# Small loads moved from POOL's queue to ACT's and SP's, and 26 shared slots where there were 24

## The chip, the cores and the metric

The kernel runs on one core of a Trainium2 chip. The metric is the device time of one execution in microseconds (us), the median of several runs. The core has five engines with instruction streams of their own: TensorE (PE; its weight loads are shown as PEld), VectorE (DVE), ScalarE (ACT), GpSimd (POOL) and SyncE (SP). Each stream runs in order. A load from memory is issued by an instruction of one of these streams and carried out by 16 DMA engines that all of them share; the issuing engine goes on meanwhile. In the profile, SPq or ACTq is the issuing side of an engine.

## What is computed

Two layers of a decoder on 256 tokens of 1024 features, in float32. Each layer is a mixer of three attention branches (A, B, C), gated and summed, an output projection and a layer norm, and then a mixture of 32 experts of which each token uses two, with a second layer norm:

```python
for l in range(DEPTH):
    mix = token_mixer(x, w_in[l], q_norm_g[l], w_uq[l], kv_norm_g[l], w_ukv[l], w_gate[l],
                      b_gate[l], w_a[l], w_b[l], w_c[l], w_o[l], cos_m, sin_m, cos_p, sin_p)
    x = layer_norm(alpha * x + mix, ln1_g[l], ln1_b[l])
    ffn = hier_moe(x, w_group[l], b_group[l], w_sub[l], b_sub[l], w1[l], w3[l], w2[l])
    x = layer_norm(alpha * x + ffn, ln2_g[l], ln2_b[l])
# token_mixer: merged = g0 * (o_a @ w_a) + g1 * (o_b @ w_b) + g2 * (o_c @ w_c); return merged @ w_o
# hier_moe: for e in range(32): y += combine[:, e] * ((silu(t @ w1[e]) * (t @ w3[e])) @ w2[e])
```

The expert weights are 3 MB each, 96 MB a layer, and all of them are read.

## The kernel before

**Slots.** Most of the on-chip memory is a pool of NSLOT = 24 slots (line 48) of 8 KiB on each of 128 partitions, which the stream of weights shares with the large temporaries of the mixer (class Slots, from line 116). One slot holds 1 MB, a whole weight tile of an expert.

**The weights' stream.** Ring (from line 166) has all weights in the order of their use. A first, dry pass over the program notes how many slots the temporaries hold after each change and where each weight is last used. In the real pass `pump` issues the next weight (L195, or L193 where a tile is gathered from four experts) as soon as `fits` finds that until the weight's last use no more than NSLOT slots would be held. All of them are issued from SP. The program's order is the order in which the Python code is written out: a load stands on SP's stream at the place at which `pump` issued it, and waits there for whoever used its slot last.

**The stages.** `setup` (line 294) issues nine loads from SP: the first part of the constants, the first half of x, the first weight, the second half of x, three more weights, the rest of the constants, and the masks (L326). Then it calls `load_small(0, ...)`, and then has ACT load a function table (L1356, `self.table`). The mixer's first actions follow: transposes of x (L519), their split into a high and a low part (L278 on ACT, L279 on DVE), the split of the first weights by the same two lines, and the first products (L283 to L285).

**Experts.** `moe` goes through the 32 experts in eight steps of four (e = 0, 4, ... 28). A step multiplies gathered rows by w1 and w3 (L1691), then by w2 (L1771), and gathers the rows of the next step (L1650). After each kind of product its weights' slots are given back, and `pump` issues more weights there. In layer 0 the end of step e = 8 calls `load_small(1, ...)` for the next layer; the router's weights go to a slot taken for them (tile wr). At e = 16, `overflow` (L1860) holds three loads of SP in a branch that is taken only when an expert has more than 32 tokens; the branch isn't taken here. Also at e = 16 of layer 0, `small_T` and `small_rows` use what load_small(1) has brought. At the end of e = 20, `load_gains` fetches the gain and the bias of the second norm into a slot of their own (tile gb, L449).

**Small loads.** load_small (from line 398) clears a tile of vectors (L402, on POOL) and issues eleven loads: seven of vectors into it (L403 to L410), the router's weights w_group and w_sub behind other data of a slot or into a slot of their own (L413, L414; rows of 16 and 128 bytes), and two biases (L416, L417). L1326 issues two loads of 4 KB (tile gpk) some way ahead of the experts. All of these, and load_gains, issue from POOL.

Of the kernel before, what the change touches and what calls it, by code (L numbers as in the profile page):

```python
# [44 lines left out]
# Columns of the output projection, and of the last experts' second product: the last ones are few, as a norm waits for them.  # L45
WO = [(0, 512), (512, 256), (768, 256)]

NSLOT = 24
T1 = 5

# Splits of weights run so many pieces ahead of their products.
# [4 lines left out]
# The steps of the last layer's end.  # L56
# [5 lines left out]
# The piece by which a queue of attention steps is to be through, and the tensor work left for what lies between two steps.  # L62
# [53 lines left out]
class Slots:  # L116
    """8 KiB slots that the weight stream and the large temporaries share."""
# [23 lines left out]
    def part(self, name, n):  # L141
        """One of n parts of a slot."""
        for p in self.shared[n]:
            if p["free"]:
                return Part(self, n, p, p["free"].pop())
        p = {"tile": self.alloc([P, n, 2048 // n], F32, name), "free": set(range(1, n))}
        self.shared[n].append(p)
        return Part(self, n, p, 0)
# [17 lines left out]
class Ring:  # L166
    """Weights in the order of their use, each loaded as soon as a slot can be spared until then.

    `plan` is what a dry pass over the program has found: the slots that its temporaries hold after
    each change, and the change at which each weight tile is released."""  # L170
# [43 lines left out]
class Dry:  # L214
    """Stands for every object of the language in the dry pass."""
# [13 lines left out]
class Trunk:  # L229
# [27 lines left out]
    def tap(self, name, ap):  # L257
        if name in self.dbg:
            self.nc.gpsimd.dma_start(self.dbg[name], ap)
# [5 lines left out]
    def evac(self, out, in_, n):  # L265
        """PSUM to SBUF on the engine of the two that has less to do."""
# [7 lines left out]
    def split(self, hi, lo, src, n):  # L274
        """src = hi + lo exactly, each of 12 significant bits."""
# [11 lines left out]
    def warm(self, n, src):  # L287
        """Products that nobody reads: the tensor engine's clock falls to half when it has little to do."""
# [109 lines left out]
    def load_small(self, l, home, o):  # L398
        """The layer's vectors, off the weights' queue; the router's weights behind the first o floats of a slot."""
        nc, a = self.nc, self.a  # L400
        v = self.v = self.t([P, P], F32, "vec", 1)
        nc.gpsimd.memset(v, 0.0)  # L402
        nc.gpsimd.dma_start(v[0:2], a["q_norm_g"][l].rearrange("(k p) -> k p", p=P))  # L403
        nc.gpsimd.dma_start(v[2:3], a["kv_norm_g"][l:l + 1])
        nc.gpsimd.dma_start(v[3:27], a["b_gate"][l].rearrange("(k p) -> k p", p=P))
        nc.gpsimd.dma_start(v[27:35], a["ln1_g"][l].rearrange("(k p) -> k p", p=P))
        nc.gpsimd.dma_start(v[35:43], a["ln1_b"][l].rearrange("(k p) -> k p", p=P))
        m = max(l - 1, 0)
        nc.gpsimd.dma_start(v[43:51], a["ln2_g"][m].rearrange("(k p) -> k p", p=P))
        nc.gpsimd.dma_start(v[51:59], a["ln2_b"][m].rearrange("(k p) -> k p", p=P))  # L410
        self.wgs = home
        self.wgb = home[:, o:o + KD * 72].rearrange("p (k f) -> p k f", k=KD)
        nc.gpsimd.dma_start(self.wgb[:, :, 36:40], a["w_group"][l].rearrange("(k p) f -> p k f", p=P))  # L413
        nc.gpsimd.dma_start(self.wgb[:, :, 40:72], a["w_sub"][l].rearrange("(k p) f -> p k f", p=P))  # L414
        self.br = self.t([1, 36], F32, "br", 1)
        nc.gpsimd.dma_start(self.br[:, 0:4], a["b_group"][l:l + 1])  # L416
        nc.gpsimd.dma_start(self.br[:, 4:36], a["b_sub"][l:l + 1])  # L417

    def small_T(self):
        """The vectors with their features on partitions; the router's weights with the gain of its input taken in."""  # L420
# [14 lines left out]
    def small_rows(self):  # L435
        """Sums over the features: what a token's mean and the input's bias add to its logits."""
# [9 lines left out]
    def load_gains(self, l, which, rows=P):  # L446
        gb = self.slots.alloc([P, 2, D], F32, "gb")
        for j, n in enumerate(("g", "b")):
            self.nc.gpsimd.dma_start(gb[:rows, j], self.a[f"ln{which}_{n}"][l:l + 1].broadcast_to([rows, D]))  # L449
        return gb  # L450

    def spread_gains(self, gb):
        """The first partition's rows to all."""
# [8 lines left out]
    def step(self, f, need=None, cost=0.45, key=None, after=()):  # L462
        """An attention step: what it needs marked, its tensor time, and steps that must lie some tensor time back."""
# [18 lines left out]
    def run_fg(self, budget):  # L482
        """Attention steps worth so much tensor time, the most urgent first."""
# [7 lines left out]
    def run_fg_until(self, mark):  # L491
        """Everything of a branch that is left, other branches' steps where it would wait."""
# [6 lines left out]
    def rate(self, i):  # L499
        """Tensor time of attention steps that a piece must be joined by for all to be done when due."""  # L500
# [29 lines left out]
    def pieces(self, l):  # L530
        """The mixer's dense products in order: each is (key of its weights, last use, prepare, product)."""
# [67 lines left out]
        def gates(br, q):  # L599
            """Two 128-column tiles of a branch's gate."""  # L600
# [26 lines left out]
        def outp(br, w, kt, i, need):  # L627
            """A branch's output columns, gated and summed: 256 or 512 columns at a time."""
# [108 lines left out]
    def rope(self, v, t, nh, half, c, s):  # L737
        """Rotates the leading dims of [128, heads, dims] in place."""
# [13 lines left out]
    # -- branch A --  # L752
# [73 lines left out]
    # -- attention units: (block 0, four heads) or (block 1, two heads), 512 scores a row --  # L826
# [1123 lines left out]
```

## Time and profile before

| | before |
|---|---|
| median of 3 runs | 1023.01 us (1022.1 to 1024.78) |
| span of the profiled execution | 1022.9 us |
| TensorE busy | 955.5 us, 93% |
| DVE, ACT, POOL busy | 473.9, 416.6, 161.7 us |
| loaded from memory | 282.44 MB, 277 GB/s over the span |

The profile is of one execution. Its page gives the busy time of each engine, the span cut into 40 slices with a digit for the busy share of each (9 is 90% or more), and the chain of work that ended last, followed back from the end. Other views of the same trace list instructions in order of time with the idle time ahead of them and what ended it, sum up waits, or cut the trace into stretches. Times in the trace are counted from the start of the span. The mixer of layer 0 runs to about 290 us, its experts to about 500; layer 1 takes the same steps from there.

### The profile page before, as it was taken

Reading aid. Unit: us, or ns where it says so; the run is one execution under the profiler, and the core shown is the slowest. Engines: PE = TensorE matmul, PEld = TensorE weight load, DVE = VectorE, ACT = ScalarE, POOL = GpSimd, SP = SyncE. Lnnn points to the kernel's source line nnn. Section 1 sums busy time; section 2 is a strip of 40 time slices with the busy share of each in tenths; the row PEclk is TensorE's granted clock in tenths of the full one; section 3 lists DMA queues with packets and bytes.
Section 4 is the critical chain, followed back from the end, with each engine's and each line's share of the span. In section 5 each row is a group of like instructions: output and inputs, shape, how many; then the busy total and the mean of one; then the engine's idle time right before and its main releaser. Section 6 shows DMA issues by size and latency. Waiting matters only on the chain.

```text
span 1022.9 us, 18674 instructions
## 1 busy us (share of the span) xinstructions
PE 955.5 (93%) x7584; PEld 770.8 (75%) x7591; DVE 473.9 (46%) x968; ACT 416.6 (41%) x911; POOL 161.7 (16%) x274
## 2 busy tenths in 40 slices
PE   8999999999999997879879999999999999977794
PEld 7888899899986774556469888998999867654462
DVE  5747776845642110111398586676455420101014
ACT  5545646644442221112345646665354422211131
POOL 4531210021100110000156071000311000000001
PEclk9999999999999998889989999999999999989898
DMA  9933261696969999999992134426968799999993
GB/s 330 328 103 124 79 210 42 220 340 216 365 241 380 417 400 419 418 417 375 376 340 68 64 124 128 162 90 224 330 232 321 288 379 420 419 419 417 419 370 121
DMA packets 100170, 284.76 MB, mean 278 GB/s; under 512 B 6324, under 2 KB 53808, under 8 KB 78576
## 3 DMA queue, kind: packets, MB, share of 16 engines
q1 hardware_dynamic: 99088, 283.12, 73.7%
q8 instruction: 62, 1.02, 0.4%
q0 software_dynamic: 992, 0.39, 0.2%
q14 instruction: 28, 0.23, 0.1%
HBM read 282.44 MB, written 1.05 MB: 277 GB/s over the span
## 4 chain that ended last, share of the span: by engine, by line
PE 68%; DMA 17%; issue 7%; POOL 3%; DVE 3%; SPq 1%; ACT 1%; POOLq 0%; DVEq 0%; ACTq 0%
DMA w<-in_w_dram 15%; PE bank L283 12%; PE bank L284 12%; PE bank L285 12%; PE bank L1650 7%; PE bank L1691 7%; PE bank L837 3%; PE bank L1771 3%; DMA w<-in_w_in_dram 2%; PE bank L891 2%; PE bank L878 2%; PE bank L1757 1%; PE bank L840 1%; PE bank L1459 1%; DVE xTl L279 1%
## 5 line engine op out<-in xcount | busy, mean ns | idle before, releaser
L279 DVE TENSOR_TENSOR ws<-w,ws 128x1024 fp32r<-128x1024 f32 (+2 forms) x154 | 184.7, 1208 | 133.1 <-ACT ws L278 124.2
L278 ACT ACTIVATE ws<-w 128x1024 fp32r<-128x1024 f32 (+2 forms) x158 | 159.0, 1023 | 35.5 <-PE bank L285 15.9
L1691 PE MATMUL bank<-w,xg 128*32 128x256 f32 x2048 | 139.6, 413 | 33.9 <-DMA w<-in_w_dram 24.4
L1691 PEld LDWEIGHTS bank<-w,xg 128*32 128x32 f32 x2048 | 70.2, 118 | 105.1 <-DMA w<-in_w_dram 30.5
L1650 PEld LDWEIGHTS bank<-xg,x 128*128 128x128 f32 x512 | 124.2, 334 | 3.0 <-issue 2.5
L1650 PE MATMUL bank<-xg,x 128*128 128x128 f32 x512 | 125.7, 399 | 0.0
L283 PE MATMUL bank<-ws,xTh 128*128 128x408 f32 (+3 forms) x320 | 116.6, 364 | 1.2 <-ACT xTh L278 1.2
L1654 ACT ACTIVATE xg<-bank,gpk 128x128 f32<-128x128 f32 x128 | 51.7, 454 | 159.3 <-PE bank L1650 159.3
L283 PE MATMUL bank<-xTh,ws 128*128 128x256 f32 x384 | 111.2, 290 | 0.0
L285 PE MATMUL bank<-ws,xTl 128*128 128x408 f32 (+3 forms) x320 | 110.6, 346 | 0.6 <-DVE xTl L279 0.6
L284 PE MATMUL bank<-ws,xTh 128*128 128x408 f32 (+3 forms) x320 | 110.3, 345 | 0.0
L284 PE MATMUL bank<-xTl,ws 128*128 128x256 f32 x384 | 108.6, 283 | 0.0
L285 PE MATMUL bank<-xTh,ws 128*128 128x256 f32 x384 | 108.5, 283 | 0.0
L1721 DVE SCALAR_TENSOR_TENSOR t<-t,cw,bank 128x256 f32<-128x256 f32 x16 | 10.8, 677 | 157.2 <-PE bank L1691 157.2
L283 PEld LDWEIGHTS bank<-xTh,ws 128*128 128x128 f32 x384 | 73.5, 191 | 1.8 <-issue 1.0
L284 PEld LDWEIGHTS bank<-xTl,ws 128*128 128x128 f32 x384 | 73.6, 192 | 0.2
L285 PEld LDWEIGHTS bank<-xTh,ws 128*128 128x128 f32 x384 | 73.5, 191 | 0.0
L283 PEld LDWEIGHTS bank<-ws,xTh 128*128 128x128 f32 x320 | 61.4, 192 | 8.1 <-ACT xTh L278 1.8
L853 ACT ACTIVATE p<-bank,nb 128x128 f32<-128x128 f32 (+1 forms) x92 | 37.3, 420 | 69.9 <-DVE nb L845 65.1
L285 PEld LDWEIGHTS bank<-ws,xTl 128*128 128x128 f32 x320 | 61.0, 191 | 5.9 <-DVE xTl L279 1.6
L284 PEld LDWEIGHTS bank<-ws,xTh 128*128 128x128 f32 x320 | 61.3, 192 | 3.4 <-DVE ws L279 0.3
L1771 PE MATMUL bank<-w,t 128*32 128x512 f32 (+1 forms) x544 | 59.1, 571 | 1.0 <-DVE t L272 1.0
(361 smaller groups left out, 1530.2 us busy)
## 6 DMA issues: line engine op xcount, KB each, us to landing
w<-in_w_dram SPq DMA_DIRECT2D x168, 1024.0 KB, 15.7
w<-in_w_gate_dram SPq DMA_DIRECT2D x24, 1024.0 KB, 5.3
w<-in_w_dram SPq DMA_DIRECT2D x80, 256.0 KB, 7.2
w<-in_w_in_dram SPq DMA_DIRECT2D x18, 1024.0 KB, 7.7
w<-in_w_in_dram SPq DMA_DIRECT2D x12, 816.0 KB, 12.8
w<-in_w_o_dram SPq DMA_DIRECT2D x8, 1024.0 KB, 8.8
w<-in_w_a_dram SPq DMA_DIRECT2D x4, 1024.0 KB, 6.1
w<-in_w_c_dram SPq DMA_DIRECT2D x4, 1024.0 KB, 5.1
```

Source lines behind the costliest of these rows:

```text
L278: self.nc.scalar.activation(hi, src, AF.Copy)
L279: (self.nc.gpsimd if self.lo_pool else self.nc.vector).tensor_tensor(lo, src, hi.bitcast(F32), op=ALU.subtract)
L283: m(out, sh, mh, start=start, stop=False)
L284: m(out, sh, ml, start=False, stop=False)
L285: m(out, sl, mh, start=False, stop=stop)
L837: nc.tensor.matmul(b[:, j * w:(j + 1) * w], q[:, blk * P:(blk + 1) * P], k[:, 0:w], start=j == 0, stop=False)
L853: nc.scalar.activation(p[:, j], v[:, j], AF.Exp, bias=nb[:, j:j + 1], scale=u["scale"], accum_out=sm[:, j:j + 1])
L878: nc.tensor.transpose(ps[:, n * P:(n + 1) * P], p[:, j * P:(j + 1) * P], self.ident)
L1650: nc.tensor.matmul(ps[:, i * P:(i + 1) * P], self.xn[:, t, k + i], pm[:, t, j:j + Q].rearrange("p e c -> p (e c)"), start=t == 0, stop=t = ...
L1654: nc.scalar.activation(xg[:, k + i], ps[:, i * P:(i + 1) * P], AF.Identity, bias=b, scale=g)
L1691: nc.tensor.matmul(hp[i * CAP:(i + 1) * CAP, c * 256:(c + 1) * 256], xg[:, k, i * CAP:(i + 1) * CAP], w[i], start=k == 0, stop=k == KD - 1 ...
L1771: nc.tensor.matmul(yp[q * CAP:(q + 1) * CAP, :w], hT[:, j, q * CAP:(q + 1) * CAP], w2[q][:, j], start=j == 0, stop=j == 1, tile_position=( ...
```

## The change

The eleven loads of load_small issue from ACT for layer 0 and from SP for layer 1; the clearing of their tile stays on POOL. The loads of load_gains and of gpk issue from SP. No load is issued from POOL any more, and the area in which POOL's queue keeps its descriptors is set to 64 bytes a partition (it had been left at its default). NSLOT goes from 24 to 26. Comments and docstrings are taken out as well.

```diff
-NSLOT = 24
+NSLOT = 26
...
     def load_small(self, l, home, o):
...
+        eng = nc.sync if l else nc.scalar
         v = self.v = self.t([P, P], F32, "vec", 1)
         nc.gpsimd.memset(v, 0.0)
-        nc.gpsimd.dma_start(v[0:2], a["q_norm_g"][l].rearrange("(k p) -> k p", p=P))
+        eng.dma_start(v[0:2], a["q_norm_g"][l].rearrange("(k p) -> k p", p=P))
...
-        nc.gpsimd.dma_start(self.wgb[:, :, 36:40], a["w_group"][l].rearrange("(k p) f -> p k f", p=P))
-        nc.gpsimd.dma_start(self.wgb[:, :, 40:72], a["w_sub"][l].rearrange("(k p) f -> p k f", p=P))
+        eng.dma_start(self.wgb[:, :, 36:40], a["w_group"][l].rearrange("(k p) f -> p k f", p=P))
+        eng.dma_start(self.wgb[:, :, 40:72], a["w_sub"][l].rearrange("(k p) f -> p k f", p=P))
         self.br = self.t([1, 36], F32, "br", 1)
-        nc.gpsimd.dma_start(self.br[:, 0:4], a["b_group"][l:l + 1])
-        nc.gpsimd.dma_start(self.br[:, 4:36], a["b_sub"][l:l + 1])
+        eng.dma_start(self.br[:, 0:4], a["b_group"][l:l + 1])
+        eng.dma_start(self.br[:, 4:36], a["b_sub"][l:l + 1])
...
     def load_gains(self, l, which, rows=P):
...
-            self.nc.gpsimd.dma_start(gb[:rows, j], self.a[f"ln{which}_{n}"][l:l + 1].broadcast_to([rows, D]))
+            self.nc.sync.dma_start(gb[:rows, j], self.a[f"ln{which}_{n}"][l:l + 1].broadcast_to([rows, D]))
...
-                    nc.gpsimd.dma_start(self.gpk[:, j * KD:(j + 1) * KD], self.a[n][l].rearrange("(p k) -> p k", p=P))
+                    nc.sync.dma_start(self.gpk[:, j * KD:(j + 1) * KD], self.a[n][l].rearrange("(p k) -> p k", p=P))
...
-    nc = _bacc.Bacc("TRN2", target_bir_lowering=False, num_devices=1)
+    nc = _bacc.Bacc("TRN2", target_bir_lowering=False, num_devices=1, dynamic_dma_scratch_size=64)
```

## Rows read from the trace of the kernel before

**Rows 1.** The page: busy time, the chain by engine and line, DMA queues.
```profile
PE 955.5 (93%) x7584; PEld 770.8 (75%) x7591; DVE 473.9 (46%) x968; ACT 416.6 (41%) x911; POOL 161.7 (16%) x274
...
q1 hardware_dynamic: 99088, 283.12, 73.7%
...
q0 software_dynamic: 992, 0.39, 0.2%
...
DMA w<-in_w_dram 15%; PE bank L283 12%; PE bank L284 12%; PE bank L285 12%; PE bank L1650 7%; PE bank L1691 7%; PE bank L837 3%; PE bank L1771 3%; DMA w<-in_w_in_dram 2%; PE bank L891 2%; PE bank L878 2%; PE bank L1757 1%; PE bank L840 1%; PE bank L1459 1%; DVE xTl L279 1%
```
**Rows 2.** The chain in order of time: start, duration, what.
```profile
382.34 19.87 DMA w<-in_w_dram
402.27 19.89 DMA w<-in_w_dram
```
**Rows 3.** SP's loads of line 195 from 360.8 to 382.3: duration ns, first and last start.
```profile
L195 SPq DMA_DIRECT2D w<-in_w_dram x8: 327/328/328, 360.7 to 379.8; - x8
```
**Rows 4.** Stretches: length, busy time by engine, granted clock, DMA share, GB/s.
```profile
298.20:303.80 5.60, 5.60 (x75) 3.92 (x74) 0.42 (x1) 3.47 (x8) 0.00 (x0) 1.00 0.25 57
806.40:811.70 5.30, 5.30 (x73) 3.45 (x72) 0.42 (x1) 3.09 (x8) 0.00 (x0) 1.00 0.28 74
346.00:366.00 20.00, 19.42 (x188) 13.76 (x184) 2.27 (x4) 4.85 (x13) 0.00 (x0) 1.00 1.01 419
```
**Rows 5.** SP's loads of line 195 from 427.3 to 437.5, as in rows 3.
```profile
L195 SPq DMA_DIRECT2D w<-in_w_dram x2: 327/331/335, 427.2 to 437.3; - x2
```
**Rows 6.** POOL's instructions in order of time: start, duration, [idle before, what ended it].
```profile
7.20 0.54 POOL L416 DMA_DIRECT2D br<-in_b_group_dram  x1 [0.23 <-DMA vec<-in_kv_norm_g_dram]
...
18.85 1.22 POOL L340 CAST mk<-masks 128x1024 bf16<-128x1024 f32 x1 [9.97 <-DMA masks<-in_masks_dram]
...
366.67 0.94 POOL L413 DMA_DIRECT2D wr<-in_w_group_dram  x1 [28.61 <-PE bank L1771]
```
**Rows 7.** TensorE: waits of 340:500 and of 840:1000 (us, times, longest); instructions in time.
```profile
PE bank L1691 <- DMA w<-in_w_dram: 11.0, 4, 4.3
...
PE bank L1691 <- DMA w<-in_w_dram: 13.3, 6, 4.3
...
898.66 0.62 PE L1691 MATMUL bank<-w,xg 128*32 128x256 f32 x2 [3.00 <-DMA w<-in_w_dram]
901.14 1.49 PE L1691 MATMUL bank<-w,xg 128*32 128x256 f32 x9 [1.86 <-DMA w<-in_w_dram]
...
958.50 1.06 PE L1691 MATMUL bank<-w,xg 128*32 128x256 f32 x2 [4.26 <-DMA w<-in_w_dram]
961.05 1.50 PE L1691 MATMUL bank<-w,xg 128*32 128x256 f32 x12 [1.49 <-DMA w<-in_w_dram]
```
**Rows 8.** SP's waits over the span: us in total, times, longest.
```profile
SPq L195 <- PE bank L1691: 62.5, 15, 14.3
```
**Rows 9.** SP's one load of line 195 at 301.4, after the hole: issue to landing.
```profile
DMA to landing us min/median/max: 4.8/4.8/4.8
```
**Rows 10.** ACT's and DVE's first instructions, in the same form.
```profile
0.77 1.28 ACT L1356 ACT_TABLE_LOAD   x1 [0.64 <-PEq L1937]
...
5.94 1.09 ACT L278 ACTIVATE xTh<-bank 128x512 fp32r<-128x512 f32 x2 [3.67 <-PE bank L519]
7.77 1.69 ACT L278 ACTIVATE ws<-w 128x832 fp32r<-128x832 f32 x2 [0.75 <-DMA w<-in_w_in_dram]
...
8.70 1.96 DVE L279 TENSOR_TENSOR ws<-w,ws 128x832 fp32r<-128x832 f32 x2 [0.84 <-ACT ws L278]
```
**Rows 11.** TensorE's first product of the mixer, in the same form.
```profile
10.04 0.44 PE L283 MATMUL bank<-ws,xTh 128*128 128x416 f32 x1
```
**Rows 12.** Stretches, as in rows 4.
```profile
10.00:46.00 36.00, 36.00 (x201) 34.55 (x200) 27.99 (x51) 22.11 (x41) 12.88 (x28) 1.00 0.98 346
517.40:524.20 6.80, 3.90 (x15) 3.64 (x16) 6.31 (x8) 3.62 (x9) 3.54 (x2) 0.50 1.03 370
```
**Rows 13.** TensorE between the layers, in order of time.
```profile
520.29 1.99 PE L1507 MATMUL bank<-cst,x 128*128 128x128 f32 x8 [5.45 <-DVE x L1495]
```

More of the change, by code (lines that the diff above doesn't have):

```diff
@@ L258, in tap @@
         if name in self.dbg:
-            self.nc.gpsimd.dma_start(self.dbg[name], ap)
+            self.nc.sync.dma_start(self.dbg[name], ap)
     def note(self, eng, n, psum=False):
@@ L400, in load_small @@
         nc, a = self.nc, self.a
+        eng = nc.sync if l else nc.scalar
         v = self.v = self.t([P, P], F32, "vec", 1)
         nc.gpsimd.memset(v, 0.0)
-        nc.gpsimd.dma_start(v[0:2], a["q_norm_g"][l].rearrange("(k p) -> k p", p=P))
[L404 to L407, printed above, removed]
+        eng.dma_start(v[0:2], a["q_norm_g"][l].rearrange("(k p) -> k p", p=P))
+        eng.dma_start(v[2:3], a["kv_norm_g"][l:l + 1])
+        eng.dma_start(v[3:27], a["b_gate"][l].rearrange("(k p) -> k p", p=P))
+        eng.dma_start(v[27:35], a["ln1_g"][l].rearrange("(k p) -> k p", p=P))
+        eng.dma_start(v[35:43], a["ln1_b"][l].rearrange("(k p) -> k p", p=P))
         m = max(l - 1, 0)
-        nc.gpsimd.dma_start(v[43:51], a["ln2_g"][m].rearrange("(k p) -> k p", p=P))
-        nc.gpsimd.dma_start(v[51:59], a["ln2_b"][m].rearrange("(k p) -> k p", p=P))
+        eng.dma_start(v[43:51], a["ln2_g"][m].rearrange("(k p) -> k p", p=P))
+        eng.dma_start(v[51:59], a["ln2_b"][m].rearrange("(k p) -> k p", p=P))
         self.wgs = home
         self.wgb = home[:, o:o + KD * 72].rearrange("p (k f) -> p k f", k=KD)
-        nc.gpsimd.dma_start(self.wgb[:, :, 36:40], a["w_group"][l].rearrange("(k p) f -> p k f", p=P))
-        nc.gpsimd.dma_start(self.wgb[:, :, 40:72], a["w_sub"][l].rearrange("(k p) f -> p k f", p=P))
+        eng.dma_start(self.wgb[:, :, 36:40], a["w_group"][l].rearrange("(k p) f -> p k f", p=P))
+        eng.dma_start(self.wgb[:, :, 40:72], a["w_sub"][l].rearrange("(k p) f -> p k f", p=P))
         self.br = self.t([1, 36], F32, "br", 1)
-        nc.gpsimd.dma_start(self.br[:, 0:4], a["b_group"][l:l + 1])
-        nc.gpsimd.dma_start(self.br[:, 4:36], a["b_sub"][l:l + 1])
+        eng.dma_start(self.br[:, 0:4], a["b_group"][l:l + 1])
+        eng.dma_start(self.br[:, 4:36], a["b_sub"][l:l + 1])
     def small_T(self):
```

## The prediction

> **What bounds the kernel now.** I read the page first: TensorE is busy for 93% of the span, so what moves the time is either a stretch in which TensorE waits, or the moment at which it starts. The chain of work gives 15% to the landing of expert weights (w from in_w_dram) [rows 1]. In order of time these are links of some 20 us that join end to end: a weight issued at 382.34 lands 19.87 later, and with its landing the one at 402.27 is issued [rows 2]. SP issues eight weights between two such ends [rows 3]: SP never has more than **eight loads on their way**, and 19.93 / 8 = 2.49 us is what one 1 MB weight takes at 419 GB/s [rows 4]. The eight are places handed out in program order: where the source has three loads in a branch that doesn't run (the overflow path), SP issues nothing from 427.2 to 437.3, as if three places were taken [rows 5]. POOL's queue has an eight of its own: its tenth load, L416, waits 0.23 us for its second to land [rows 6].
>
> The waits of TensorE on these weights are 11.0 us in layer 0 (340 to 500) and 13.3 in layer 1 (840 to 1000) by the waits view, in pairs of which two are shown [rows 7]. Before the experts the DMA engines have a hole in either layer, though there is work for them: 298.2 to 303.8 at 57 GB/s and 806.4 to 811.7 at 74 [rows 4]. There SP waits for a slot that the first experts' products (L1691) still hold, 14.3 us at the longest [rows 8]. So: too few slots ahead of the experts, then bandwidth, and TensorE pays at the end of that stream.
>
> **Two more slots.** Each lets one more weight be issued before the hole. Two weights take 2 x 2.49 = 4.98 us, and the holes are 5.6 and 5.3 us long at less than a fifth of the rate, so both fit: the stream runs 4.98 us ahead from there, and is limited by bandwidth afterwards, not by slots. TensorE's last wait of the stream (958.50 and 961.05, 5.75 us together) ends with a landing [rows 7], so it ends 4.98 earlier; the first pair of waits in layer 1 (898.66 and 901.14, 4.86) should be gone. What comes after is TensorE's own work. **Layer 1: -5.0** (bounds -3, if they fit the hole only in part, to -7.5, one weight more, if later short stops fill too). Layer 0 would give the same but for the next step. By the Trainium skill ("DMA: Bandwidth & Descriptors", Specifications) HBM gives one core some 358 GB/s; two slots would then be worth an estimated 5.9 us a layer. The row has 419, and the measurement decides.
>
> **Small loads on SP, layer 0's experts.** load_small(1) puts eleven loads among the weights, at the end of the third four experts. On POOL they cost the weights' queue nothing: L413 could sit 28.61 us on its slot [rows 6]. On SP each takes one of the eight places. POOL's issue at 366.67 shows when the slot is free; SP, whose places come free every 2.49 us, has more weights to issue before that point than it had (the two of the new slots), so I cost the slot at nothing; if SP did wait there, eight loads on their way, 20 us, would cover it. But places come free one every 2.49 us. Loads 1 to 8 are issued as eight weights land, no weight meanwhile, and when the eighth has landed **nothing large is on its way**. Loads 9 to 11 wait for loads 1 to 3, which lie behind the same weights; only then comes a weight, and one alone takes 4.8 us to land [rows 9], 4.8 - 2.49 = 2.3 over its own time. Three issues take between 3 x 0.33 (SP's weights [rows 3]) and 3 x 0.94 us (POOL's issue of the router's weights [rows 6]); I take 1.9, as one of them is of that scattered kind. How long after the last weight a small load lands no row shows: 0 to 2, and I take 0.3, as it has stood in line all the time. Drain: 2.3 + 1.9 + 0.3 = 4.5 (3.3 to 7.1). Of the lead of 4.98 remains **layer 0: -0.5** (+2.1 to -1.7). The two loads of the gains, later in both layers, and the two of gpk ahead of the experts take two of eight places: six weights, 15 us, stay on their way. Nothing; without that cover 0.4 each.
>
> **Small loads on ACT, the start.** load_small(0) stands behind nine loads of SP in the source and ahead of ACT's first work (a table load, then the halves of x and of the first weight). No row shows a load issued by ACT, so the cost has two ends. Low end: ACT has places of its own, pays only its issues. High end: ACT's loads go with SP's kind of queue (the page's q1 hardware_dynamic; POOL's is q0 software_dynamic [rows 1]) and **share SP's eight**. Then ACT's first takes the place of SP's second load, its eighth that of the ninth, the masks, and each waits for that landing. The masks land at 18.8, as POOL's wait for them shows [rows 6]; SP's landings before matter less, since ACT stands in line. I take the high end: places are given in program order even to loads that don't run [rows 5], and the profile has one eight per kind. Step by step: 18.8; four issues (two of 0.7, two of 0.4) 2.2, so 21.0; table load 1.28 and a dummy of 0.2, 22.5; the copies of x 1.09, 23.6; the first half weight 0.85, 24.4; DVE's part 0.98, 25.4. Before, these began at 0.77, 5.94, 7.77 and 8.70 [rows 10], and TensorE's first product came at 10.04 [rows 11]. From there to 46 us TensorE is never idle [rows 12], so the delay stays: 25.4 - 10.0 = **+15.4** (four issues of 0.33 to 0.94: 14.5 to 17). Then the clock: after the wait of 5.45 us that ends at 520.29 [rows 13] the granted clock is 0.50, the lower of its two levels (1.2 of 2.4 GHz), until 524.2 [rows 12]. That is some 4 us of work at half speed, 2 lost. After the wait of 15 us I take **+1.7** (0 to 3.4, twice that). SP's next weights take places behind ACT's and come some 2 us late; hidden, as their products come 15 us late; otherwise they would cost those 2. What POOL is spared, eleven issues of about 0.5, lies in its idle time: 0. Nothing downstream takes the delay back: the weights of the mixer wait for slots that TensorE frees, so they move with it.
>
> The 64-byte area only makes room; POOL issues nothing any more. **Sum** on the profiled execution, span 1022.9, 0.1 from the median of 1023.01 of the runs (which have nothing to add around it): 1022.9 + 15.4 + 1.7 - 0.5 - 5.0 = **1034.5**.
>
> **Rivals.** 1. *ACT has places of its own*: this ends on the faster side. ACT issues eleven loads from about 1.0 on (behind POOL's clearing of their tile) in 9 x 0.4 + 2 x 0.9 = 5.4 us, its table load ends at 7.9, the copies start at 7.9 and not 5.94, the first half weight at 9.0 and not 7.77: +1.2 (0 to 4). 1022.9 + 1.2 - 5.5 = 1018.6, faster by 0.4%. It decides when ACT's eighth load doesn't wait for the masks. For it: no row has ACT's loads; against it: two kinds of queue, two eights. The Trainium skill's rule that loads of several engines run on the same 16 DMA engines, and that issuing from another engine saves or costs only the issue ("DMA: Bandwidth & Descriptors", Issuing engines are not separate DMA queues), would come out here; it says nothing of places, and no row of this trace tests it. 2. *Shared places, but SP doesn't drain* (the small loads land between weights and give places back): layer 0 keeps its 5.0: 1022.9 + 17.1 - 10 = 1030. Against it: in [rows 2] a load's landing frees just the place eight further on, so the small ones' turn comes behind the weights. 3. *The slots bring no lead* (the planner or the slots' order can't use them, so the change doesn't do that part): 1022.9 + 17.1 + 4.5 = 1044.5. Against it: in the hole SP waits for a slot [rows 8].
>
> **How the numbers follow.** Forecast 0.70 (itself 1029 to 1038); rival 1 0.18 (1016 to 1022); rival 2 0.07; rival 3 0.05. About 0.3%, 3 us, is what a measurement of this kernel can tell from no change. Faster than 1019.9: two thirds of rival 1, 0.12. Within: its rest and a forecast gone mild, 0.08. Slower than 1026.1: 0.80. The range from 1019 to 1038 holds nine tenths of the forecast, all of rival 2 and over half of rival 1: 8 in 10.
>
> **What would show it.** ACT's table load at about 21 and not 0.77, TensorE's first product near 25, ACT's waits there on x, w and masks: step right; near 11: rival 1. The two holes filled to nearly 400 GB/s: the lead. In layer 0 a new hole of some 4.5 us near 393 (all times after the start later by its delay), behind SP's small loads, and waits on weights as long as before; in layer 1 the wait pair at 898 gone. If layer 0's waits shrink by 5 there is no drain; if both layers keep theirs and the holes too, the slots bring nothing. I am wrong as a whole if the start is unmoved.

## The result, and the profile after

The changed kernel takes 1053.38 us (1052.19 to 1055.64), the kernel before 1023.89 us in the same comparison (1022.1 to 1025.21). The ratio is 1.0275, with an interval from 1.0244 to 1.0306. Slower was the right direction, but the time lies 19 us above the forecast of 1034.5 and 15 above the upper end of the range. The profiled executions have spans of 1053.9 and 1022.9 us, 31.0 apart.

First the page of the kernel after: busy times, DMA queues (packets, MB, share), chain by line.

```profile
PE 967.9 (92%) x7590; PEld 775.2 (74%) x7591; DVE 473.7 (45%) x968; ACT 415.8 (39%) x911; POOL 142.6 (14%) x244
...
q1 hardware_dynamic: 101862, 283.33, 71.5%
...
q10 hardware_dynamic: 2190, 0.18, 0.2%
...
DMA w<-in_w_dram 22%; PE bank L283 13%; PE bank L284 13%; PE bank L285 12%; PE bank L1692 5%; PE bank L1651 5%; PE bank L838 3%; PE bank L892 2%; PE bank L879 2%; PE bank L1772 2%; DMA gb<-in_ln_g_dram 1%; PE bank L841 1%; PE bank L1758 1%;
```

Beside [rows 1]: q0, POOL's queue, is gone; q10, ACT's, is new. The landing of expert weights has risen from 15% to 22% of the chain, which is the wrong way for a change that gives the weights more slots, and a name that was not there has come in: gb, the gains of the second norm. (From the changed lines on, a line number of after is one higher: L1692 is L1691 of before, L1772 is L1771, L459 is L458, L450 is L449.)

Where the 31.0 us lie is read by the start of the same TensorE instruction in both traces. The first row is [rows 11]; those that carry most weight are shown below.

| instruction of TensorE | before | after | difference |
|---|---|---|---|
| first product of the mixer | 10.04 | 16.80 | +6.8 |
| experts of layer 0, second weights | 304.48 | 313.26 | +8.8 |
| free for the gains' product, layer 0 | 478.74 | 484.06 | +5.3 |
| starts it | 478.74 | 495.07 | +16.3 |
| last four experts, second product | 497.83 | 518.73 | +20.9 |
| free for the gains' product, layer 1 | 984.31 | 1000.75 | +16.4 |
| starts it | 984.31 | 1011.52 | +27.2 |
| last four experts, second product | 1003.41 | 1034.67 | +31.3 |

So: start +8.8; experts of layer 0, up to the gains, -3.5; the gains' wait +11.0 and what follows it +4.6; the mixer of layer 1 and its experts up to the gains -4.5; the gains again +10.8 and +4.1. The gains' part alone, 30.5 us, is as large as the whole net loss: two loads of 4 KB a layer, for which the prediction said "Nothing".

**The gains.** TensorE in order of time (start, duration, [idle before, what ended it]) in layer 0, and the same product in layer 1:

```profile
480.42 3.64 PE L1772 MATMUL bank<-w,t 128*32 128x512 f32 x32
495.07 7.16 PE L459 MATMUL bank<-gb,one 1*128 1x512 f32 x8 [11.01 <-DMA gb<-in_ln_g_dram]
502.16 6.45 PE L1692 MATMUL bank<-w,xg 128*32 128x256 f32 x64
...
1011.52 7.16 PE L459 MATMUL bank<-gb,one 1*128 1x512 f32 x8 [10.77 <-DMA gb<-in_ln_g_dram]
```

In the kernel before this product follows w2's without a gap and takes 3.70 us, and the 64 products after it take 5.35:

```profile
478.74 3.70 PE L458 MATMUL bank<-gb,one 1*128 1x512 f32 x8
482.36 5.35 PE L1691 MATMUL bank<-w,xg 128*32 128x256 f32 x64
```

In the kernel after they take 7.16 and 6.45. The windows of the kernel after say why (length, busy time by engine, granted clock, DMA share, GB/s):

```profile
484.00:495.00 11.00, 0.06 (x4) 0.00 (x0) 0.69 (x1) 0.60 (x1) 0.00 (x0) 0.65 1.03 372
495.00:502.20 7.20, 7.13 (x12) 2.53 (x14) 1.38 (x2) 0.60 (x1) 0.00 (x0) 0.50 1.08 365
502.20:508.60 6.40, 6.40 (x66) 2.91 (x65) 0.00 (x0) 0.60 (x1) 0.00 (x0) 0.56 1.07 374
```

TensorE stood idle for 11 us, and then its granted clock is 0.50, the lower of its two levels. The DMA engines are busy all the time (372 GB/s): what TensorE waits for is not bandwidth but its turn. SP's stream shows the turn. Its loads of line 193 from 464 to 489.2 (count, duration ns, first and last start):

```profile
L193 SPq DMA_DIRECT2D w<-in_w_dram x18: 327/328/661, 464.4 to 488.6; - x18
```

and SP in order of time right behind them:

```profile
489.32 0.42 SPq L450 DMA_DIRECT2D gb<-in_ln_g_dram  x1
```

Eighteen loads of the last four experts' weights stand ahead of the gains on SP's stream, and they go as places come free: one per 2.49 us as long as loads of 1 MB hold the places (to 481.8). These eighteen are smaller themselves, sixteen of 256 KB and two of 512, so from there they go one per 0.7 us. POOL, which had nothing else to do, had issued the gains at 449.31 in the kernel before:

```profile
449.31 0.55 POOL L449 DMA_DIRECT2D gb<-in_ln_g_dram  x1 [11.45 <-PE bank L1771]
```

SP gets there at 489.32, five us after TensorE needs them.

**The start.** ACT and TensorE of the kernel after, in order of time:

```profile
3.29 0.34 ACTq L411 DMA_DIRECT2D vec<-in_ln_b_dram  x1
7.19 0.41 ACTq L414 DMA_DIRECT2D masks<-in_w_group_dram  x1
...
8.35 4.80 ACTq L417 DMA_DIRECT2D br<-in_b_group_dram  x1
...
13.49 1.28 ACT L1357 ACT_TABLE_LOAD   x1 [13.36 <-DMA br<-in_b_group_dram]
...
14.89 1.07 ACT L278 ACTIVATE xTh<-bank 128x512 fp32r<-128x512 f32 x2
...
16.80 0.71 PE L283 MATMUL bank<-ws,xTh 128*128 128x416 f32 x1 [6.29 <-ACT ws L278]
```

ACT issues seven loads by 3.6, then stands for 3.6 us until a place is free, then 4.80 us in the issue of 16 bytes (L417). Its table load comes at 13.49 instead of 0.77, its first copy at 14.89 instead of 5.94 [rows 10], TensorE's first product at 16.80 instead of 10.04 [rows 11]. Behind it, after the wait of 6.29 us, the granted clock is 0.50 (16.8 to 20.0), and by the sixteenth product the delay has grown to 9.9 us (22.88 against 12.95).

An issue that takes long is not new. In the kernel before one of SP takes 4.13 us (L322, the rest of the constants), where the same one takes 0.34 in the kernel after:

```profile
5.13 4.13 SPq L322 DMA_DIRECT2D cst<-in_consts_dram  x1
```

**Slots and drain.** The loads of whole expert weights that SP has issued before the hole ahead of layer 0's experts (line and tile: count, duration ns, first and last start). The kernel before, up to 300 us:

```profile
L195 SPq DMA_DIRECT2D w<-in_w_dram x18: 327/328/442, 228.7 to 286.7; - x18
```

The kernel after, up to 309 us:

```profile
L195 SPq DMA_DIRECT2D w<-in_w_dram x20: 328/328/433, 232.0 to 295.5; - x20
```

Two weights more: the lead is there. But the hole is there too, as the windows of the kernel after show (columns as in [rows 4]; the second row is used below):

```profile
306.80:312.40 5.60, 5.60 (x75) 4.10 (x75) 0.42 (x1) 3.47 (x8) 0.00 (x0) 1.00 0.20 44
...
398.90:406.30 7.40, 1.93 (x28) 0.63 (x16) 0.00 (x0) 0.38 (x1) 0.00 (x0) 0.94 0.78 230
```

44 GB/s over 5.6 us, against 57 in [rows 4]. In layer 0's experts SP's small loads do what the prediction said of them; SP, and last TensorE, in order of time:

```profile
381.57 0.30 SPq L404 DMA_DIRECT2D vec<-in_q_norm_g_dram  x1
...
396.53 0.27 SPq L411 DMA_DIRECT2D vec<-in_ln_b_dram  x1
398.95 0.41 SPq L414 DMA_DIRECT2D wr<-in_w_group_dram  x1
...
400.85 5.84 SPq L195 DMA_DIRECT2D w<-in_w_dram  x9
...
406.34 6.56 PE L1692 MATMUL bank<-w,xg 128*32 128x256 f32 x58 [5.04 <-DMA w<-in_w_dram]
```

From 381.57 to 396.53 there is one small load per 2.49 us, each in the place of a landed weight; at 398.95 the last weight lands, at 400.85 the next one is issued, and TensorE has it at 406.34. In between the DMA engines move 230 GB/s where the stream has 419 [rows 4]. The waits on expert weights (340 to 500, 840 to 1000, as in [rows 7]: us, times, longest) are nevertheless shorter in both layers than the 11.0 and 13.3 of before:

```profile
PE bank L1692 <- DMA w<-in_w_dram: 7.3, 4, 5.0
...
PE bank L1692 <- DMA w<-in_w_dram: 9.6, 6, 3.2
```

### The profile page after: what moved, and what is told of

It reads as the page before. It is cut to its first block, busy times and chain, and to the rows that moved or that the text cites. A ratio compares the mean times of both kernels' runs of the same rounds, so it can differ in the third digit from the quotient of the medians.

```text
span 1053.9 us, 18657 instructions
## 1 busy us (share of the span) xinstructions
PE 967.9 (92%) x7590; PEld 775.2 (74%) x7591; DVE 473.7 (45%) x968; ACT 415.8 (39%) x911; POOL 142.6 (14%) x244
## 4 chain that ended last, share of the span: by engine, by line
PE 64%; DMA 24%; issue 5%; POOL 3%; DVE 2%; ACT 1%; ACTq 1%; SPq 1%; POOLq 0%; DVEq 0%
DMA w<-in_w_dram 22%; PE bank L283 13%; PE bank L284 13%; PE bank L285 12%; PE bank L1692 5%; PE bank L1651 5%; PE bank L838 3%; PE bank L892 2%; PE bank L879 2%; PE bank L1772 2%; DMA gb<-in_ln_g_dram 1%; PE bank L841 1%; PE bank L1758 1%; DVE xTl L279 1%; PE bank L459 1%
## 5 line engine op out<-in xcount | busy, mean ns | idle before, releaser
L1692 PE MATMUL bank<-w,xg 128*32 128x256 f32 x2048 | 140.9, 417 | 26.5 <-DMA w<-in_w_dram 17.0
L1692 PEld LDWEIGHTS bank<-w,xg 128*32 128x32 f32 x2048 | 69.6, 119 | 101.1 <-issue 27.7
L283 PE MATMUL bank<-ws,xTh 128*128 128x408 f32 (+3 forms) x320 | 117.8, 368 | 7.5 <-ACT ws L278 6.3
L285 PE MATMUL bank<-ws,xTl 128*128 128x408 f32 (+3 forms) x320 | 111.7, 349 | 0.8 <-DVE xTl L279 0.8
L284 PE MATMUL bank<-ws,xTh 128*128 128x408 f32 (+3 forms) x320 | 111.4, 348 | 0.3 <-DVE ws L279 0.3
L285 PE MATMUL bank<-xTh,ws 128*128 128x256 f32 x384 | 108.5, 283 | 0.0
L1722 DVE SCALAR_TENSOR_TENSOR t<-t,cw,bank 128x256 f32<-128x256 f32 x16 | 10.8, 675 | 152.6 <-PE bank L1692 152.6
L285 PEld LDWEIGHTS bank<-xTh,ws 128*128 128x128 f32 x384 | 73.5, 191 | 0.0
L285 PEld LDWEIGHTS bank<-ws,xTl 128*128 128x128 f32 x320 | 61.9, 193 | 6.1 <-DVE xTl L279 1.8
L1772 PE MATMUL bank<-w,t 128*32 128x512 f32 (+1 forms) x544 | 59.1, 571 | 1.0 <-DVE t L272 1.0
```

The source lines that it names most:

```text
L283: m(out, sh, mh, start=start, stop=False)
L284: m(out, sh, ml, start=False, stop=False)
L285: m(out, sl, mh, start=False, stop=stop)
L1692: nc.tensor.matmul(hp[i * CAP:(i + 1) * CAP, c * 256:(c + 1) * 256], xg[:, k, i * CAP:(i + 1) * CAP], w[i], start=k == 0, stop=k == KD - 1 ...
L1772: nc.tensor.matmul(yp[q * CAP:(q + 1) * CAP, :w], hT[:, j, q * CAP:(q + 1) * CAP], w2[q][:, j], start=j == 0, stop=j == 1, tile_position=( ...
```

## The experiments

Ratios are to the kernel before, measured on the same chip; 0.0010 is one us.

### The gains, moved and undone

**e1_gains_early.** The changed kernel; only the place of the gains' load in the program differs.

```diff
-            if e == NE - 3 * Q:
+            if e == 4 * Q:
                 self.gb2 = self.load_gains(l, 2, 1)
```

> The changed kernel with one edit: the two loads of the second norm's gain and bias stand on SP's stream four experts' steps earlier (end of e = 16, not e = 20), so that 18 loads of the last experts' weights no longer stand ahead of them. Theory (the gains' loads wait behind those weights, TensorE waits 11.0 and 10.8 us for them at L459, and the low clock after the wait loses 4 to 5 us more each time): 1053.4 - 31 = about 1022.5, no wait at L459. Rival (the weights themselves are that late, and the wait would come back a few us later at the last experts' products): 1035 or more, with waits of L1692 or L1772 on w in its place.

Measured: 1024.73 us, ratio 1.0003 (0.9985 to 1.002). SP issues the gains at 452.81, 32 us ahead of the product, which has no gap before it and its old lengths after it:

```profile
452.81 0.28 SPq L450 DMA_DIRECT2D gb<-in_ln_g_dram  x1
...
484.87 3.69 PE L459 MATMUL bank<-gb,one 1*128 1x512 f32 x8
488.49 5.32 PE L1692 MATMUL bank<-w,xg 128*32 128x256 f32 x64
```

So the place of the gains' two loads in the order of the source is 28 us of the changed kernel (1.0275 against 1.0003), nearly all that it lost.

**e2_b_gains_sp.** The reverse: the kernel before with nothing but the gains' load on SP.

```diff
-            self.nc.gpsimd.dma_start(gb[:rows, j], self.a[f"ln{which}_{n}"][l:l + 1].broadcast_to([rows, D]))
+            self.nc.sync.dma_start(gb[:rows, j], self.a[f"ln{which}_{n}"][l:l + 1].broadcast_to([rows, D]))
```

> The kernel before with one part of the change alone: the gains' loads issue from SP, 24 slots, all other small loads from POOL. With 24 slots 12 loads of the last experts' weights stand ahead of them, not 18. Theory: they would land at about 485 and 992, TensorE waits some 6 us in layer 0 and 8 in layer 1, and 3 to 4.5 each for the low clock: 1023.9 + 20 to 23 = 1044 to 1047. Rival (the gains matter only together with the other parts): 1024.

Measured: 1036.27 us, ratio 1.0118 (1.0094 to 1.0141). The mechanism is there alone, but it costs 12 us, not 20 to 23. SP's loads of line 193 ahead of the gains, from 455 to 479:

```profile
L193 SPq DMA_DIRECT2D w<-in_w_dram x12: 327/328/328, 457.7 to 478.3; - x12
```

and the gains' product on TensorE's timeline:

```profile
482.06 7.16 PE L458 MATMUL bank<-gb,one 1*128 1x512 f32 x8 [2.59 <-DMA gb<-in_ln_g_dram]
```

Twelve loads stand ahead, not eighteen: with 24 slots the stream of weights runs less far ahead of the program, and so the gains stand less far behind. The wait is 2.59 us in layer 0 and 4.33 in layer 1; the low clock after it is the same.

**h1_after_24.** The changed kernel with `NSLOT = 24`, to see whether the slots and the gains' delay hang together.

> The changed kernel with 24 slots instead of 26, its gains' load left late on SP's stream. With the early load the two slots were worth 11.9 us (1036.6 against 1024.7). Theory (the late load costs less with 24 slots, since 12 loads of weights stand ahead of it and not 18: it cost 12.4 where it stood alone): 1036.6 + 12.4 = 1049 us, so the two slots are worth only some 4 us of the changed kernel; gains issued near 479 + 13 us, a wait at their product of 2 to 5 us. Rival (the costs add up whatever the slots): 1053.4 + 11.9 = 1065 us.

Measured: 1049.70 us, ratio 1.0240 (1.0216 to 1.0263), as the theory had it, and not 1065. Twelve loads ahead of the gains again, and waits of 3.73 us in layer 0 (below) and 4.75 in layer 1:

```profile
494.87 6.93 PE L459 MATMUL bank<-gb,one 1*128 1x512 f32 x8 [3.73 <-DMA gb<-in_ln_g_dram]
```

In the kernel as changed the two slots therefore bring nothing (1.0275 with, 1.0240 without; the intervals overlap): what they win is lost again, because the lead that they give to the weights is a longer line ahead of the gains.

**g2_gains_act.** The changed kernel with the gains' load on ACT's queue (`self.nc.scalar.dma_start` in load_gains), at the same place of the program. It asks whether the line is SP's stream or the places.

> The changed kernel with the gains' load on ACT's queue instead of SP's, at the same place of the program. Theory (the gains came late since SP issues them behind 18 weights' loads that wait for places): ACT comes to the issue at about 459 us, 24 us ahead of the product, they land in time and nothing waits on them, so 1024.7 us as with the early load, at most 5 more where ACT's issue stalls. Rival (the eight places, shared by both queues, hold it back): the wait at the gains' product stays over 5 us and the time is over 1035.

Measured: 1075.80 us, ratio 1.0482 (1.0445 to 1.052), 21 us worse than the change itself. The theory fell. ACT comes to the load early, as expected, and then stands there (ACT, then TensorE, in order of time):

```profile
457.39 0.60 ACT L278 ACTIVATE y<-bank 128x512 fp32r<-128x512 f32 x1 [1.20 <-PE bank L1772]
488.06 0.47 ACTq L450 DMA_DIRECT2D gb<-in_ln_g_dram  x1
489.35 0.22 ACTq L450 DMA_DIRECT2D gb<-in_ln_b_dram  x1
489.62 0.38 ACT L1717 ACTIVATE t<-bank 128x256 f32<-128x256 f32 x1 [31.64 <-DMA w<-in_w_dram]
...
490.06 6.41 PE L1692 MATMUL bank<-w,xg 128*32 128x256 f32 x64 [23.37 <-ACT t L1717]
```

ACT is through with its copies at 458.0, and its issue goes at 488.06, released by the landing of a weight that SP issued: almost the moment at which SP issued it in the changed kernel (489.32). While ACT stood, SP issued seventeen loads of line 193 (463.96 to 487.36), so the places are not given to whoever comes first. A slot still in use can hardly be what ACT waited for: TensorE, which reads the weights out of the slots, had stood idle since 466.69. Both queues draw from **one set of places in one set order**, and in that order the gains stand behind the same weights, whoever issues them. In layer 1 the trace shows the wait as a semaphore instruction of 32.44 us ahead of an issue of 0.46: it is the program that waits for a place. Whether the chip would take more than eight loads at once no run shows. On ACT it is worse, since ACT's next instruction (L1717) and with it TensorE wait as well, 23.37 us in layer 0 and 23.99 in layer 1.

The Trainium skill says of loads started from several engines that this saves only the sequencer's time to start them, which is usually small relative to the load itself ("DMA: Bandwidth & Descriptors", Issuing engines are not separate DMA queues). The two issues agree with it, at 0.47 and 0.22 us. What the engine pays here is the wait for a place ahead of them, 30 us in this run.

**g1_fill.** The changed kernel with 36 products that nobody reads in the gains' wait.

```diff
+                self.warm(36, self.mk)
                 self.spread_gains(self.gb2)
```

> The changed kernel with 36 products that nobody reads (128x512, three of which take 0.82 us at the full clock) ahead of the gains' product, in the wait of 11 us, in both layers. Theory (what follows the wait costs another 4.5 us a layer, because the clock is 0.50 after an idle TensorE): the gains' products take 3.6 us again instead of 7.16 and the first products of expert 28 take 5.3 instead of 6.45, so 1053.4 - 9 = 1044 to 1046 us. Rival (the time after the wait is lost to weights that come late, as the slots were held): 1053, with the same products as long as before or with waits on weights in their place.

Measured: 1048.94 us, ratio 1.0247 (1.022 to 1.0273), 2.9 us better than the change by the ratios and 4.4 by the medians, with overlapping intervals: less than the theory's 7 to 9. TensorE's timeline (span 1046.1) shows the effect, and that it is partial:

```profile
485.00 7.94 PE L291 MATMUL bank<-mk 128*128 128x512 bf16 x35
494.31 4.85 PE L459 MATMUL bank<-gb,one 1*128 1x512 f32 x8 [1.36 <-DMA gb<-in_ln_g_dram]
499.09 5.80 PE L1692 MATMUL bank<-w,xg 128*32 128x256 f32 x64
```

and the window of the gains' product:

```profile
494.00:499.00 5.00, 4.69 (x8) 1.57 (x8) 1.38 (x2) 0.60 (x1) 0.00 (x0) 0.77 1.07 374
```

The gains' products take 4.85 us and not 7.16, the next 64 take 5.80 and not 6.45, at a granted clock of 0.77 where it was 0.50. No weight is waited for in their place, so the rival is out, in the trace; that the whole of the 4.6 and 4.1 us after the waits is the clock's is likely but not shown by the time.

### The start

**e3_b_small0_act.** The kernel before with layer 0's small loads on ACT.

```diff
+        eng = nc.gpsimd if l else nc.scalar
-        nc.gpsimd.dma_start(v[0:2], a["q_norm_g"][l].rearrange("(k p) -> k p", p=P))
+        eng.dma_start(v[0:2], a["q_norm_g"][l].rearrange("(k p) -> k p", p=P))
...
```

> The kernel before with one part alone: layer 0's eleven small loads issue from ACT. Theory (ACT and SP share eight places, ACT's first work begins at about 13.5 and not 0.8, and nothing gives the delay back): 1023.9 + 8.8 = 1032.7, TensorE's first product near 17. Rival (the delay is made good before the experts end, as TensorE waits for weights there): 1024 to 1027.

Measured: 1034.54 us, ratio 1.0099 (1.0074 to 1.0123). The start alone costs 10 us; the experts of layer 0 begin 9.1 us later than before (309.42 against 300.32). The stall in L417 is there too:

```profile
8.57 5.53 ACTq L417 DMA_DIRECT2D br<-in_b_group_dram  x1
```

**f4_all_sp_early.** The changed kernel with the early gains and with all of load_small on SP (`eng = nc.sync`), so that ACT issues nothing.

> The changed kernel with layer 0's small loads on SP instead of ACT, and with the gains' load at the end of expert 16. Theory (what the start lost came of ACT's own instructions standing behind its DMA issues): ACT's table load and copies start as in the kernel before, the 10.4 us fall to what the ten loads delay SP's first weights, 2 to 5 us, so 1016 to 1019 us. Rival (the start waits on the eight places, whoever issues): 1024.7, as with the loads on ACT.

Measured: 1019.54 us, ratio 0.9947 (0.9924 to 0.997), 0.5 us above the theory's 1016 to 1019 and 5.7 us better by the ratios than with ACT as the issuer (e1). SP, ACT and TensorE in order of time:

```profile
17.44 0.58 SPq L415 DMA_DIRECT2D masks<-in_w_sub_dram  x1
...
0.75 1.28 ACT L1357 ACT_TABLE_LOAD   x1 [0.62 <-PEq L1938]
...
6.42 1.22 ACT L278 ACTIVATE xTh<-bank 128x512 fp32r<-128x512 f32 x2 [4.17 <-PE bank L520]
...
9.56 0.43 PE L283 MATMUL bank<-ws,xTh 128*128 128x416 f32 x1
```

ACT's work begins as in the kernel before and so does TensorE's. The loads still have to wait for places, now on SP, where they hold up the next weights: the experts begin at 303.35, 3.0 us later than before and not 8.8. What ACT's issues cost was ACT's own work behind them.

### Layer 1's small loads, in layer 0's experts

**e4_b_small1_sp.** The kernel before with load_small(1) on SP (`eng = nc.sync if l else nc.gpsimd`).

> The kernel before with one part alone: layer 1's eleven small loads issue from SP among the weights of layer 0's experts. Theory (eight of them take all places, and the weights' stream stands still for some 5 us): TensorE's waits on weights in layer 0 grow by 3 to 5 us, 1027 to 1029. Rival (the small loads pass between weights, or the stream makes it good as it is no longer held up by POOL's loads): 1024.

Measured: 1026.66 us, ratio 1.0025 (1.0001 to 1.005): 2.6 us by the ratio, a little under the 3 to 5 expected, and the interval nearly touches no change. The waits on weights in layer 0 are 14.2 us instead of 11.0, with one that was not so long before:

```profile
399.09 3.21 PE L1692 MATMUL bank<-w,xg 128*32 128x256 f32 x28 [7.60 <-DMA w<-in_w_dram]
```

**h2_all_sp_early2.** f4 with load_small(1) after the first four experts (`if e == 0`) instead of the third.

> All small loads on SP, 26 slots, gains' load at the end of expert 16, and layer 1's small loads issued after expert 0 instead of after expert 8. Theory (the drain of the stream by ten small loads costs less where the slots are full and TensorE is ahead of no weight): the wait of 5.95 us at expert 24 falls to the 1.6 to 3.6 of the kernel before, 1016 to 1018 us. Rival (the drain takes the same time out of the stream wherever it stands, which the weights set): 1019.5 as with the later place.

Measured: 1018.28 us, ratio 0.9949 (0.9934 to 0.9965), the same as f4 (0.9947). The wait of 5.95 us of f4 (it ends at 401.68; it lies at expert 16, not at 24 as the expectation has it) is replaced by two of 2.71 and 1.86, but a later one is longer (3.96 for 1.86). The time sides with the rival: the eleven loads take the same out of the stream in either place, as far as these intervals tell, some 2 us.

### The slots

**f1_early_24.** e1 with 24 slots: both small-load costs, none of the lead.

> The changed kernel with the gains' load at the end of expert 16, and with 24 slots instead of 26: all small loads on ACT and SP, none of the two slots more. Theory (the two slots are worth what the layers' expert waits lost): loads on ACT cost 10.4, layer 1's on SP 2.5, nothing is won back, so 1024 + 12.9 = 1036 to 1037 us; the waits of TensorE on expert weights are those of the kernel before again, 11 us in layer 0 and over 10 in layer 1. Rival (the two slots gain nothing, and the two costs overlap with something else): 1024.7, as with 26 slots.

Measured: 1036.63 us, ratio 1.0109 (1.0078 to 1.014). The two costs measured alone, 9.9 per mille (e3) and 2.5 (e4), add up to 12.4; here they are 10.9. With the early gains the two slots are worth 1.0109 - 1.0003, 10.9 us. The waits on weights (340 to 500, 840 to 1010) are 14.3 and 12.5 us; in e1 they are 7.2 and 9.7:

```profile
PE bank L1692 <- DMA w<-in_w_dram: 14.3, 4, 7.8
...
PE bank L1692 <- DMA w<-in_w_dram: 12.5, 6, 4.1
```

**f2_before_25.** The kernel before with one slot more, paid for by half of POOL's descriptor area; every small load stays on POOL.

```diff
-NSLOT = 24
+NSLOT = 25
...
+    nc = _bacc.Bacc("TRN2", target_bir_lowering=False, num_devices=1, dynamic_dma_scratch_size=8192)
```

> The kernel before with 25 slots, the one more taken out of POOL's descriptor area (16 KiB to 8 KiB); every small load stays on POOL. Theory (each slot is one weight of lead, and a hole in the stream is shortened by each): half of the two slots' 12.3 us, so 1018 us, with the wait at the first expert of layer 1's half shorter by half than before's. Rival 1 (loads wait for something else than slots): 1024. Rival 2 (a smaller area lets POOL's loads wait for one another): over 1024, with the first POOL loads later than in the kernel before.

Measured: 1018.28 us, ratio 0.9944 (0.9921 to 0.9968): 5.7 us for one slot. SP issues 19 weights before the hole, and the waits are 8.1 and 11.5 us. The half that was expected of them (the wait at the first experts of layer 1) is not how they shrink: it is spread over all.

**f3_before_26_pool.** The kernel before with 26 slots and an area of 192 bytes; only w_group and w_sub, of many short rows, go to SP.

> The kernel before with 26 slots and POOL's area at 192 bytes: of the small loads only the two matrices of the router (w_group, w_sub) go to SP, as their descriptors are the many ones; the others, gains included, stay on POOL. Theory: the full worth of the two slots without the three costs, 1024 - 12 = 1012 us, less up to 2.5 where SP's two loads a layer drain the stream. Rival (a small area lets POOL's loads wait for one another, so that gains or the start come late): 1024 or more, with a wait at the gains' product or at the first copies.

Measured: 1016.61 us, ratio 0.9935 (0.9915 to 0.9955), the best ratio of all, though not to be told from f2 by these intervals. Expected was 12 us, found 6.7. POOL's nine loads are out by 9.3 us, with two pauses of 1.5 us between them, TensorE starts as in the kernel before, and the waits on weights are 7.8 and 10.3 us, hardly less than with 25 slots. The trace of f3 has one thing that f2's has not, in the experts of layer 0 (SP in order of time, then a window of the DMA engines):

```profile
375.88 11.02 SPq L414 DMA_DIRECT2D wr<-in_w_sub_dram  x1
...
387.00:392.00 5.00, 4.58 (x75) 2.27 (x68) 1.38 (x2) 0.60 (x1) 0.00 (x0) 1.00 0.86 200
```

SP's issue of w_sub takes 11.02 us, in which no weight is issued, and behind it the DMA engines move 200 GB/s where the stream has 419. Part of the second slot's worth can have gone there; that was not tried.

## Why the prediction was wrong, step by step

**The gains, the failing step.** "The two loads of the gains ... take two of eight places: six weights, 15 us, stay on their way. Nothing" costs the load by what it takes from the weights, and asked nothing about what the weights take from it. Its reader, a product of TensorE, has a due time of its own, and the prediction did not ask for it. Counting the loads of weights between its place in the source and its product would have shown the delay. In the kernel before these are twelve (e2), SP's first twelve of line 193 there:

```profile
L193 SPq DMA_DIRECT2D w<-in_w_dram x12: 327/328/328, 458.0 to 478.7; - x12
```

TensorE is free for the product at 478.74, so a load behind the twelfth comes late even there, and with two slots more it stands behind eighteen. Measured: 11.0 and 10.8 us of waiting, 4.6 and 4.1 after it, 28 us by e1. The step looked at the weights behind the load on SP's stream, and not at those ahead of it.

**The start, right in kind, mis-sized.** Predicted +15.4 and +1.7 for the clock; measured +6.8 at the first product and +8.8 at the experts. That ACT shares SP's places holds (in g2 ACT's issue is released by the landing of one of SP's weights). The step that failed is "its eighth that of the ninth, the masks": the order of the places is not that of the source. ACT's eighth load goes at 7.19, when a weight lands, and SP issues the masks only at 12.18. In place of the wait for the masks stands one that the prediction had no term for, 4.80 us in the issue of 16 bytes; that an issue can take so long the trace of before showed on SP (4.13 us at L322, 5.12 for a weight of the mixer), in rows that the prediction didn't use. The clock's term was there: some 3 us are lost behind the first product, waits of 0.3 included, and 1.1 are won back before the experts, where the prediction had nothing downstream take the delay back. The value lies between the two ends given, 1.2 and 15.4, and I took the end. Rival 1, places of ACT's own, is out.

**The slots, the right size by a wrong reason.** Layer 1's experts gained 4.5 us up to the gains, where -5.0 was predicted. But the lead was not loaded in the hole, as the prediction had it. SP waits there for a slot as before, and the hole stands (44 GB/s); the two weights were issued before it, 20 for 18, while the mixer still ran. That the stream stops for slots earlier too stands in the part of SP's waits that [rows 8] leaves out: the same line waits 192.1 us for the mixer's products (L285) in the kernel before, 203.4 in the kernel after.

**The drain.** Predicted 4.5 us; the rows give (406.34 - 398.95) - 2.49 = 4.9. At TensorE's end it is smaller, 2.6 us in e4, where the waits of layer 0 grow by 14.2 - 11.0 = 3.2 in all. With that, layer 0 should have kept some -2; it kept -3.5, and the rest is not explained.

**The sum.** Predicted 17.1 - 0.5 + 0 - 5.0 = 11.6; measured 8.8 - 3.5 + 15.6 - 4.5 + 14.9 = 31.3 up to the last experts. Without the gains it would have been 0.8, and e1, which is that kernel, is at 1024.73: neither the forecast nor its sign would have held, so that the sign came out right was luck. The two other errors, a start costed twice too high and a drain too dear, would have shown then.

## What to carry to other kernels

A load that is moved into another stream must be costed from its reader: count what stands ahead of it there, at the rate at which that goes, and compare the landing with the time at which the reader comes. The deeper a prefetch runs, the longer that line is, so a change that deepens it and a change that joins its line are not additive: here the same two slots were worth 11 us with the gains out of the line and nothing with them in it. An engine that has work of its own is a poor issuer of loads, as a load that waits for its place holds up everything behind it; a small part of a freed resource (one slot, with the idle queue left alone) gave nearly all that was to be had, 5.7 us.

## What the runs showed of the hardware

- Loads of ACT and SP go by the same places in this program: ACT's issue in g2 stood for 30 us until a weight issued by SP had landed, and the wait is one of the program's semaphores (32.44 us in layer 1). That the chip itself stops at eight is not shown. That a separate queue (q10 beside q1 on the page) doesn't mean separate places was half expected; that moving a load to a quiet engine could cost 21 us was not.
- One issue on ACT, of 16 bytes, took 4.80 us (5.53 in e3), where its neighbours took 0.27 to 0.67. It does not belong to that load: from SP it took 0.43 in f4 and 0.42 in layer 1 of the changed kernel. SP has such issues too: in the kernel before 4.13 us (L322) and 5.12 (a weight of the mixer, w_in), in f3 11.02 (w_sub). Why they are long was not tried and stays open.
- After a wait of 11 us TensorE's granted clock was 0.50; products in the wait raised it to 0.77 in the stretch behind.
- With POOL's descriptor area cut to 192 bytes, nine small loads of layer 0 still went out by 9.3 us, with pauses of 1.5 us ahead of two of them.
